# Weaving W1's units between W2's K tile pairs in a two-layer decoder trunk

## The chip, the cores and the metric

The kernel runs on one core of a Trainium2 chip. The metric is the time of one execution on the device, in microseconds (us). Five engines matter by name: TensorE (PE in the profile, its weight loads PEld), VectorE (DVE), ScalarE (ACT), GpSimd (POOL, almost unused) and SyncE (SP), which issues the DMAs. Each engine works through its own queue in order; semaphores tell it when an operand is there or a buffer free.

## The reference

Two decoder layers over 256 positions of width 2048, all in float32. Layer 0 mixes with a gated short convolution, layer 1 with multi-head latent attention; behind each mixer stands the same feed-forward block, and behind every sub-layer a layer norm of `alpha * x + f(x)`:

```python
def sq_relu_mlp(x, w1, w2):
    return jnp.square(jax.nn.relu(x @ w1)) @ w2
...
    h = layer_norm(ALPHA * h + mix, ln_g[layer, 0], ln_b[layer, 0])
    h = layer_norm(ALPHA * h + sq_relu_mlp(h, mlp_w1[layer], mlp_w2[layer]),
                   ln_g[layer, 1], ln_b[layer, 1])
```

W1 is 2048 x 8192 and W2 8192 x 2048. The change concerns this feed-forward block alone.

## The kernel before, in words

**Numbers in two parts.** TensorE multiplies in a rounded format (F32R). To keep float32's accuracy each operand is split: `split` (L125) casts the number to `hi` on ScalarE (L127) and takes the rest `lo` on VectorE (L128). A product is then hi by hi, hi by lo and lo by hi.

**Weights.** Every weight is read from memory once, as tiles of 128 x 1024 float32 (512 KB), in one fixed order, the list `stream`. `take` (L183) hands the next tiles to the matmuls and keeps `LOOK` = 5 preparation steps ahead. `prepare` (L141) does a step: a DMA on SP into one of `RAW` = 5 raw tiles, then the split into one of `WA` = 8 pairs of hi and lo tiles. So preparing weights is work for ScalarE and VectorE all through the kernel.

**The feed-forward block** (`mlp`, L575). The 8192 hidden columns are done in eight passes of 1024 (`NQ` = 8). A pass q has eight *units*: unit m is `x @ W1` for 128 hidden columns, 16 K tiles of one 512-column and one 256-column matmul (`mm_run`, L221: `high` L215 with the hi weights against x's hi and lo parts, `low` L219 with the lo weights). `whole` (L352) adds the two halves of the sum, ScalarE applies relu and square, and two units together are split into the tile `h`. In one K tile of a pass's first unit, number `TURNED` = 2, `low` stands ahead of `high`; that is the *turned* K tile.

The second half of the pass multiplies `h` by its 1024 rows of W2 and adds onto the running sums `acc`, 256 x 2048. The first and the last pass (q = 0, 7) do this plainly (`down`, L313). The middle passes (`FAST`, q = 1 to 6) use a Strassen-like scheme of **seven products** instead of eight: a *K tile pair* j (two hidden tiles) and a *column group* g (two of the four 512-column blocks) make a 2 x 2 by 2 x 2 block product, which `fast_products` (L343) does with seven accumulators named in `FACTORS` ("3", "1", "5", "7", "2", "6", "4"), each three matmuls (`dot`, L297: L300, L302, L303). For it, VectorE forms sums of the blocks of `h` (`form`, L703, into `sf` and `forms`), and `prepare` makes three split tiles and a half one out of two raw tiles, with one 1024-column and two 512-column differences (`raw_t` L162, L166, L169). The four accumulators in `OWN` have sums of their own (`sums`), which `fold` adds into `acc` after pass 6.

A middle pass is thus four pairs by two groups. Group 1 is done as `MIXED` = "sssp": three pairs by seven products and the fourth, the *plain* pair, by eight (`down_pairs`, L634), with one matmul cut in two (`EVEN`). Then group 0 is done, four pairs by seven products. In the profile the accumulators of group 1 are `ps_r`, those of group 0 `ps_f`, the units `ps_u`. A group's running sums are copied into the accumulators by ScalarE (`resumed`, L612; `resume` spreads those of group 1 over units 3 to 7), and copied back by ScalarE (`put_back`, L616) or added by VectorE (`keep`, L624).

The eight PSUM banks change roles from pass to pass: `busy` holds four banks for the units and part of the sums, `free` the other four.

In layer 0's last pass the next norm's preparation (`ln.prepare`, called by `begin`) goes along with the units; in layer 1 `turn_residual` (called by `extra`) transposes the residual behind the first unit of passes 1 to 4. The order on each engine follows the program's order as the tile framework schedules it; it moves independent instructions past each other.

Of the kernel before, what the change touches and what calls it, by code (L numbers as in the profile page):

```python
# [16 lines left out]
P = 128  # L17
# [20 lines left out]
MIXED = "sssp"  # L38
EVEN = (QC - 1, "22")
# [14 lines left out]
def trunk(ctx: ExitStack, tc: tile.TileContext, xT, vecs, lead, w_first, w_in, w_out, w_kv, w_q, w_uk, w_uv,  # L54
# [27 lines left out]

    def mlp_stream(l):
        out = []
        for q in range(NQ):
            out += halves(w1[l, q * QC:(q + 1) * QC])
            if q not in FAST:
                out += halves(w2[l, q])
                continue
            for j, kind in enumerate(MIXED):  # L90
                out += [(w2f[l, q, 1, j, 0], w2f[l, q, 1, j, 1])] if kind == "s" else \
                    halves(w2[l, q, 2, j]) + halves(w2[l, q, 3, j])
            out += [(w2f[l, q, 0, j, 0], w2f[l, q, 0, j, 1]) for j in range(QC // 2)]
        return out
# [480 lines left out]
    def mlp(idx, ln, blocks, fast, begin=None, extra=None, last=False):  # L575
# [32 lines left out]
        def resumed(p, g, name, bank):  # L608

            ps = psum(name, bank)  # L610
            if q != FAST[0] or p not in OWN:
                nc.scalar.copy(ps, place(p, g))  # L612
            return ps

# [3 lines left out]
        def keep(p, g, ps):  # L618

            at = place(p, g)  # L620
            if q == FAST[0] and p in OWN:
                nc.scalar.copy(at, ps)
            else:
                nc.vector.tensor_tensor(at, at, ps, ALU.add)  # L624

        def resume(busy, free, ps, m):

            b2, b3, b4, b6 = free
            b1, b5, b7, b22 = busy
            for p, bank in {3: (("3", b3),), 4: (("2", b2),), 5: (("4", b4), ("1", b1)), 6: (("6", b6), ("5", b5)),  # L630
                            7: (("7", b7), ("22", b22))}.get(m, ()):
                ps[p] = resumed(p, 1, f"ps_r{p}", bank)

        def down_pairs(h, forms, busy, free, ps):  # L634

            b2, b3, b4, b6 = free
            b1, b5, b7, b22 = busy
            new = set(OWN) if q == FAST[0] else set()
            onto = set(ps) - new
            for j, kind in enumerate(MIXED):  # L640
                if kind == "s":
                    last = j == MIXED.rindex("s")
                    fast_products(ps, h, forms, j, new if j == 0 else (), OWN if last else (), onto)
                    if last:
                        for p in OWN:
                            put_back(p, 1, ps[p])
                        then = {p: resumed(p, 0, f"ps_f{p}", bank) for p, bank in (("3", b1), ("1", b5))}
                    continue
                for two in (((0, "2"), (1, "4")), ((1, "22"), (0, "3"))):
                    w, = take(1, LOOK + 1)  # L650
                    for t, p in two:
                        for kk in range(2):
                            k = 2 * j + kk
                            dot(ps[p], wide_rows(w, kk), held(h[k], t), False, k == QC - 1, (k, p) == EVEN, True)
                    if j == len(MIXED) - 1:
                        if "5" not in then:
                            then.update({p: resumed(p, 0, f"ps_f{p}", bank) for p, bank in (("5", b7), ("7", b6))})
                        for _, p in two:
                            put_back(p, 1, ps[p])
            n = QC // 2  # L660
            onto = set(then) - new
            then.update({p: psum(f"ps_f{p}", bank) for p, bank in (("2", b2), ("6", b4), ("4", b22))})
            for j in range(n):
                fast_products(then, h, forms, j, set(then) - onto if j == 0 else (), then if j == n - 1 else (), onto)
            for p, _, _ in FACTORS:
                (put_back if p in onto or p in new else keep)(p, 0, then[p])
            return (b3, b1, b5, b7), (b6, b2, b4, b22)

        def fold():

            s1, s5, s7, s6 = (sums[:, i] for i in range(4))
            c = acc.rearrange("p t (g b c) -> p t b g c", g=2, b=2)
            for d, a, b in ((c[:, 0, 0], c[:, 0, 0], s1), (s6, s6, s1), (c[:, 0, 1], c[:, 0, 1], s6), (s7, s7, s6),
                            (c[:, 1, 0], c[:, 1, 0], s7), (c[:, 1, 1], c[:, 1, 1], s7),
                            (c[:, 0, 1], c[:, 0, 1], s5), (c[:, 1, 1], c[:, 1, 1], s5)):
                nc.vector.tensor_tensor(d, a, b, ALU.add)
                yield
# [8 lines left out]
        busy, free = (0, 1, 2, 3), (4, 5, 6, 7)  # L686
        for q in range(NQ):
            ht = act.tile([P, QC, 2 * T], F32R, tag="c", name=f"h{idx}_{q}")
            h = [ht[:, k, :] for k in range(QC)]
            forms = None  # L690
            if q in FAST:
                forms = act.tile([P, QC // 2, 2, 4 * P], F32R, tag="a2", name=f"forms{idx}_{q}")
            pair = []

            def pair_tile(m):

                if m % 2 == 0:
                    pool = (act, "ab") if m % 4 else (fast, "fp")
                    t = pool[0].tile([P, 2 * T], F32, tag=pool[1], name="fp")
                    pair.append(t.rearrange("p (i t) -> p i t", i=2))  # L700
                return pair[-1]

            def form(j):  # L703
                (a11, a21), (a12, a22) = ((pair[j][:, i, :P], pair[j][:, i, P:]) for i in range(2))
                sf = fast.tile([P, 4, P], F32, tag="sf", name="sf")
                s1, s2, s3, s4 = (sf[:, i, :] for i in range(4))
                nc.vector.tensor_tensor(s1, a21, a22, ALU.add)
                nc.vector.tensor_tensor(s3, a21, a11, ALU.subtract)
                nc.vector.tensor_tensor(s2, s1, a11, ALU.subtract)
                nc.vector.tensor_tensor(s4, a12, s2, ALU.subtract)  # L710
                split(forms[:, j, 0, :], forms[:, j, 1, :], sf.rearrange("p i c -> p (i c)"))

            def hidden(m, ps, evac, *func):
                both = pair_tile(m) if q in FAST else None
                f = both[:, m % 2, :] if both is not None else tmp.tile([P, T], F32, tag="fh", name="fh", bufs=3)
                evac(ps, f, *func)
                if not func:
                    nc.scalar.activation(f, f, AF.Relu)  # L718
                nc.scalar.activation(f, f, AF.Square)
                if both is None:  # L720
                    put_split(h[m], f)
                elif m % 2:
                    at = ht[:, m - 1:m + 1, :]
                    split(at[:, :, :T], at[:, :, T:], both)
                    form(m // 2)

            if q == 0:
                for m in range(QC):
                    if m < GROUP:
                        if m == 0:  # L730
                            ws = ln.ws if ln.ws else group_of(GROUP)
                            if not ln.ws:
                                mm_wide(ws, ln.xd)
                            ln.finish()
                        ps = ws[m][1]
                    else:
                        ws = [(take(), psum("ps_w"))]
                        mm_wide(ws, ln.xd)
                        ps = ws[0][1]
                    hidden(m, ps, ln.weighted, AF.Relu)  # L740
                acc = act.tile([P, 2, D], F32, tag="a1", name=f"acc{idx}")
            else:
                folds = fold()
                begun = {}
                for m, ps in enumerate(products(QC, xhl, TURNED, busy)):
                    hidden(m, ps, whole)
                    if extra and m == 0 and q <= NB:
                        for t in range(2):
                            extra(block, q - 1, t, busy[2 + t])
                    if q in FAST:  # L750
                        resume(busy, free, begun, m)
                    if q == NQ - 1:
                        next(folds, None)
                        if last and m >= QC - 2:
                            for t in range(2):
                                last_sum(m - QC + 2, t, free[2 * (m - QC + 2) + t])
# [19 lines left out]
    def to_wide(block, put, h):  # L776
# [10 lines left out]
        for n in range(NB):  # L787
            down(h, put, n)
            if n:
                turned(n - 1)  # L790
# [397 lines left out]
```

## Time and profile before

| what | value |
|---|---|
| median of three times | 1999.71 us (1998.16 to 2004.2) |
| span of the profiled execution | 1994.9 us, first to last instruction |
| the median over that span | 4.8 us; the profiled execution's own time is not listed beside its span |
| PE, DVE, ACT busy | 1987.7, 1709.4, 1354.9 us |
| DMA | 385.85 MB, mean 193 GB/s |
| the feed-forward passes 1 to 7 of layer 0 | from 452.78 to 997.46 us |
| of layer 1 | from 1394.56 us on |

In the rows, columns are start and length of an instruction, engine, line, operation, tile written and tiles read. A row of a stretch gives its length and then each engine's busy time with the number of instructions in brackets, the granted TensorE clock, the DMA share and GB/s. Matmuls are pipelined: their listed lengths overlap, so the start of the next one tells what one costs. To a lesser degree this holds for VectorE and ScalarE too.

### The profile page before, as it was taken

The numbers are of one execution on the slowest core, as the hardware profiler recorded it, in microseconds if no ns is written. First come the engines' busy times: TensorE is split into PE (matmuls) and PEld (weight loads), VectorE is DVE, ScalarE is ACT, GpSimd is POOL, SyncE is SP. The second block draws the span as 40 slices with busy tenths as digits, with TensorE's granted clock in tenths as the row PEclk, the third lists the DMA queues.
The fourth block names the chain that finished last, engine by engine and source line by source line (L and its number), as shares of the span: only waits on it lengthen the run. The fifth ranks groups of instructions, "written<-read, shape, count | busy, mean of one in ns | idle before, by whom it ended". The sixth has DMA issues, their size and how long they took to land.

```text
span 1994.9 us, 30180 instructions
## 1 busy us (share of the span) xinstructions
PE 1987.7 (100%) x11110; PEld 1737.2 (87%) x11110; DVE 1709.4 (86%) x2555; ACT 1354.9 (68%) x2154; POOL 2.3 (0%) x21
## 2 busy tenths in 40 slices
PE   9999999999999999999999999999999999999998
PEld 8888888988888888888889998898888888888886
DVE  8667667797999989989978988777899999999985
ACT  6444445586778778777756755558677787887772
POOL 0000000000000000000000000000000000000000
PEclk9999999999999999999999999999999999999999
DMA  8666666565657466574855543656464656656483
GB/s 318 205 191 187 190 190 190 179 193 157 212 170 251 148 216 221 177 243 147 281 171 159 170 140 123 201 180 195 146 233 155 232 161 220 222 178 233 150 269 130
DMA packets 106853, 385.85 MB, mean 193 GB/s; under 512 B 11857, under 2 KB 12625, under 8 KB 106449
## 3 DMA queue, kind: packets, MB, share of 16 engines
q1 hardware_dynamic: 106560, 383.79, 59.5%
q8 instruction: 87, 1.43, 0.3%
q14 instruction: 62, 0.50, 0.1%
q10 hardware_dynamic: 144, 0.13, 0.0%
HBM read 381.78 MB, written 2.10 MB: 192 GB/s over the span
## 4 chain that ended last, share of the span: by engine, by line
PE 98%; DVE 1%; ACT 1%; issue 0%; DVEq 0%; ACTq 0%
PE ps_u L215 20%; PE ps_l L215 13%; PE ps_u L219 10%; PE ps_l L219 7%; PE ps_f L300 4%; PE ps_f L303 4%; PE ps_f L302 4%; PE ps_r L303 4%; PE ps_r L302 4%; PE ps_r L300 4%; PE ps_d L300 2%; PE ps_d L302 2%; PE ps_d L303 2%; PE ps_w L249 2%; PE ps_w L248 2%; PE ps_w L247 2%
## 5 line engine op out<-in xcount | busy, mean ns | idle before, releaser
L128 DVE TENSOR_TENSOR lo<-raw,hi 128x1024 fp32r<-128x1024 f32 x710 | 861.8, 1220 | 190.6 <-ACT hi L127 119.9
L127 ACT CAST hi<-raw 128x1024 fp32r<-128x1024 f32 x710 | 741.8, 1051 | 247.4 <-PE ps_l L215 98.1
L215 PE MATMUL ps_u<-xhl,hi 128*128 128x512 f32 x1792 | 621.7, 392 | 0.0
L219 PE MATMUL ps_u<-xhl,lo 128*128 128x256 f32 x1792 | 498.2, 279 | 0.0
L215 PEld LDWEIGHTS ps_u<-xhl,hi 128*128 128x128 f32 x1792 | 334.5, 187 | 73.6 <-ACT acc L595 0.2
L219 PEld LDWEIGHTS ps_u<-xhl,lo 128*128 128x128 f32 x1792 | 338.1, 189 | 1.8
L215 PE MATMUL ps_l<-xhl_a,hi 128*128 128x512 f32 x704 | 244.1, 393 | 0.0
L219 PE MATMUL ps_l<-xhl_a,lo 128*128 128x256 f32 x704 | 195.4, 279 | 0.0
L215 PEld LDWEIGHTS ps_l<-xhl_a,hi 128*128 128x128 f32 x704 | 132.1, 188 | 29.9
L219 PEld LDWEIGHTS ps_l<-xhl_a,lo 128*128 128x128 f32 x704 | 131.9, 188 | 0.2
L127 ACT CAST hi_t<-raw_t 128x1024 fp32r<-128x1024 f32 x84 | 88.5, 1054 | 45.8 <-DVE raw_t L162 41.4
L162 DVE TENSOR_TENSOR raw_t<-raw,raw 128x1024 f32<-128x1024 f32 x84 | 102.3, 1218 | 1.8 <-DMA raw<-in_w2f_dram 1.5
L128 DVE TENSOR_TENSOR lo_t<-raw_t,hi_t 128x1024 fp32r<-128x1024 f32 x84 | 102.4, 1219 | 0.2
L718 ACT ACTIVATE fp<-fp 128x256 f32<-128x256 f32 x96 | 40.0, 416 | 63.2 <-DVE fp L356 62.6
L215 PE MATMUL ps_l<-z,hi 128*128 128x512 f32 x240 | 82.4, 391 | 0.0
L300 PE MATMUL ps_d<-hi,h 128*128 128x512 f32 x192 | 75.0, 391 | 0.0
L302 PE MATMUL ps_d<-lo,h 128*128 128x512 f32 x192 | 75.0, 390 | 0.0
L303 PE MATMUL ps_d<-hi,h 128*128 128x512 f32 x192 | 74.8, 389 | 0.0
L249 PE MATMUL ps_w<-xd,hi 128*128 128x258 f32 x256 | 72.7, 284 | 0.0
L248 PE MATMUL ps_w<-xd,lo 128*128 128x258 f32 x256 | 72.3, 282 | 0.0
L247 PE MATMUL ps_w<-xd,hi 128*128 128x258 f32 x256 | 72.3, 282 | 0.0
L215 PE MATMUL ps_l<-oT,hi 128*128 128x512 f32 x208 | 71.3, 391 | 0.0
(296 smaller groups left out, 3963.7 us busy)
## 6 DMA issues: line engine op xcount, KB each, us to landing
raw<-in_w_dram SPq DMA_DIRECT2D x344, 512.0 KB, 4.5
raw<-in_w2f_dram SPq DMA_DIRECT2D x168, 512.0 KB, 3.9
raw<-in_w_in_dram SPq DMA_DIRECT2D x88, 512.0 KB, 4.2
raw<-in_w_out_dram SPq DMA_DIRECT2D x32, 512.0 KB, 3.7
raw<-in_w_o_dram SPq DMA_DIRECT2D x32, 512.0 KB, 4.2
raw<-in_w_kv_dram SPq DMA_DIRECT2D x10, 512.0 KB, 3.7
raw<-in_w_q_dram SPq DMA_DIRECT2D x8, 512.0 KB, 4.0
raw<-in_w_uk_dram SPq DMA_DIRECT2D x8, 512.0 KB, 3.9
```

The lines of the kernel that those rows point to most:

```text
L127: nc.scalar.copy(hi, src)
L128: nc.vector.tensor_tensor(lo, src, hi.bitcast(F32), ALU.subtract)
L162: nc.vector.tensor_tensor(t.rearrange(two, a=2), b12.unsqueeze(1).to_broadcast([P, 2, BW]), r1.rearrange(two, a=2), ALU.subtract)
L215: nc.tensor.matmul(ps, w[blk // 8][0][:, blk % 8, :], x, start=first, stop=False)
L219: nc.tensor.matmul(ps[:, :T], w[blk // 8][1][:, blk % 8, :], x[:, :T], start=False, stop=last)
L247: nc.tensor.matmul(ps[:, :W], hi, x[k][:, :W], start=k == 0, stop=False)
L248: nc.tensor.matmul(ps[:, :W], lo, x[k][:, :W], start=False, stop=False)
L249: nc.tensor.matmul(ps[:, :W], hi, x[k][:, W:], start=False, stop=k == NC - 1)
L300: nc.tensor.matmul(ps, x[0], w[0], start=first, stop=False, skip_group_check=onto)
L302: nc.tensor.matmul(ps[:, at], x[0], w[1][:, at], start=False, stop=False, skip_group_check=onto)
L303: nc.tensor.matmul(ps, x[1], w[0], start=False, stop=last, skip_group_check=onto)
L718: nc.scalar.activation(f, f, AF.Relu)
```

## The change

**Order.** The units of a pass no longer stand together. From pass 1, unit 5 on, each unit is followed by one K tile pair of the seven-product work: `steps` yields (q, m, pair), where the pair is number m - 5 of the same pass for m = 5, 6, 7 and number m + 3 of the preceding pass for m = 0 to 4. So the pairs lag the units by `SHIFT` = 5. Five units ahead of the first pair and three behind the last stand alone. The stream of weights follows the same order: two tiles for a unit, then the two raw tiles of a pair.

**All pairs by seven products.** `PLAIN` is empty, so the plain pair and the cut matmul are gone; each of the 48 pairs of a layer takes `fast_products`. The branches for a plain pair are left in the code and unused.

**Turned tile.** `TURN` is true for every unit, so each unit of passes 1 to 7 has its third K tile turned.

**Banks and sums.** Seven banks hold the seven accumulators all through; all woven units share the eighth ("unit"), lone ones alternate between it and the bank of "6". The group changes once a pass: a group's last four pairs of one pass and first four of the next follow each other. At the change (`end`), all seven sums are put back and those of the other group resumed, all on ScalarE; `keep` is gone.

**Smaller moves.** `fold` works by group, 16 additions of 512 columns in place of 8 of 1024. Layer 0's preparations go with three lone units (chunks 1 to 9) and, chunks 10 to 15, into the block that follows. Layer 1's transposes go behind units 0 to 3 of pass 1. The function `to_wide` gains two lines for this.

The diff, cut to its core (helpers that only changed their place are left out):

```diff
-MIXED = "sssp"
-EVEN = (QC - 1, "22")
+PLAIN = ()
+SHIFT = 5
+
+
+def TURN(q, m):
+    return True
...
+    def steps():
+
+        for q in range(1, NQ):
+            for m in range(QC):
+                p, i = (q, m - SHIFT) if m >= SHIFT else (q - 1, m + QC - SHIFT)
+                yield q, m, (p, i // NB, i % NB, (p % 2) ^ (i // NB)) if p in FAST else None
...
     def mlp_stream(l):
-        out = []
-        for q in range(NQ):
-            out += halves(w1[l, q * QC:(q + 1) * QC])
...
+        out = halves(w1[l, :QC]) + halves(w2[l, 0])
+        for q, m, pair in steps():
+            out += halves(w1[l, q * QC + m])
+            if pair:
+                p, i, j, g = pair
...
+                    [(w2f[l, p, g, j, 0], w2f[l, p, g, j, 1])]
+        return out + halves(w2[l, NQ - 1])
...
+        base = Banks.count
+        bank = {p: (base + i) % 8 for i, p in enumerate(("6", "unit", "3", "1", "5", "7", "2", "4"))}
...
+        def resume(p, g, at=None):
+
+            ps[p] = psum(f"ps_{p}", bank[at or p])
+            onto.discard(p)
+            if p in OWN and begun[g] == FAST[0]:
+                fresh.add(p)
+            else:
+                nc.scalar.copy(ps[p], place(p, g))
+                onto.add(p)
...
+        def products_of(p, i, j, g):
...
+            end = i == 0 or p == FAST[-1]
...
+            fast_products(ps, h, forms, j, set(fresh), OWN if own else order if j == NB - 1 and end else (), onto)
+            fresh.clear()
...
+            elif j == NB - 1 and end:
+                begun[g] = 0
+                for o in order:
+                    put_back(o, g, ps[o])
+                    if i == 0:
+                        resume(o, 1 - g)
+            if p == FAST[-1] and j == NB - 1:
+                folds = chain(folds, fold(g))
+
+        for q, m, pair in steps():
+            lone = pair is None
+            if q == FAST[0] and m == SHIFT:
+                for o, _, _ in FACTORS:
+                    resume(o, 1)
+            w = take(2, LOOK + 1)
+            at = "6" if lone and m % 2 == 0 else "unit"
+            un = psum("ps_u", bank[at])
+            mm_run([(w, un)], xhl, 0, NC, NC, turned=TURNED if TURN(q, m) else None)
+            f = pair_tile(m)[:, m % 2, :]
+            whole(un, f)
+            nc.scalar.activation(f, f, AF.Relu)
+            nc.scalar.activation(f, f, AF.Square)
+            if extra and q == FAST[0] and m < NB:
+                for t in range(2):
+                    extra(block, m, t, spare[1 + (2 * m + t) % 3])
+            if q == NQ - 1:
+                for _ in range(3 if m >= SHIFT else 2):
+                    next(folds, None)
+                if begin and m >= SHIFT:
+                    begin(range(3 * (m - SHIFT) + 1, 3 * (m - SHIFT) + 4))
+            if pair:
+                products_of(*pair)
+            if m % 2:
+                finish_pair(m // 2)
...
+            if n < 2:
+                prepare_chunks(range(10 + 3 * n, 13 + 3 * n))
```

More of the change, by code (lines that the diff above doesn't have):

```diff
@@ L626, in resume @@
[L626 to L675, printed above, removed]
+        def fold(g):
+            s1, s5, s7, s6 = (sums[:, i, g, :] for i in range(4))
+            c = [[block(2 * g + b, t) for b in range(2)] for t in range(2)]
+            for d, a, b in ((c[0][0], c[0][0], s1), (s6, s6, s1), (c[0][1], c[0][1], s6), (s7, s7, s6),
+                            (c[1][0], c[1][0], s7), (c[1][1], c[1][1], s7), (c[0][1], c[0][1], s5), (c[1][1], c[1][1], s5)):
@@ L684, in last_sum @@
             nc.scalar.copy(finals[n, t], block(n, t))
[L686 to L690, printed above, removed]
-            if q in FAST:
[L692 to L737, printed above, removed]
@@ L738, in mlp, with finish_pair @@
+        def finish_pair(j):
+            both = fps.pop(j)
+            at = ht[:, 2 * j:2 * j + 2, :]
+            split(at[:, :, :T], at[:, :, T:], both)
+            if q in FAST:
+                form(j, both)
+        q = 0
+        for m in range(QC):
+            if m < GROUP:
+                if m == 0:
+                    ws = ln.ws if ln.ws else group_of(GROUP)
+                    if not ln.ws:
                         mm_wide(ws, ln.xd)
-                        ps = ws[0][1]
-                    hidden(m, ps, ln.weighted, AF.Relu)
@@ L741, in mlp @@
-                acc = act.tile([P, 2, D], F32, tag="a1", name=f"acc{idx}")
-            else:
[L743 to L756, printed above, removed]
-                        if begin:
-                            begin(range(max(2 * m, 1), 2 * m + 2))
@@ L760, in mlp @@
-            if q == NQ - 1 and last:
-                for i, (n, t) in enumerate(((2, 0), (3, 0), (2, 1), (3, 1))):
-                    last_sum(n, t, busy[i])
-                blocks(block, finals, h)
-                return
-            if q == NQ - 1:
-                blocks(block, put, h)
-                return
-            if q == 0:
-                for n in range(NB):
-                    down(h, put, n)
-                    if begin and n == 1:
-                        begin(range(1))
-            else:
-                busy, free = down_pairs(h, forms, busy, free, begun)
+                    ln.finish()
@@ new lines, in mlp @@
+                ps = ws[m][1]
+            else:
+                ws = [(take(), psum("ps_w"))]
+                mm_wide(ws, ln.xd)
+                ps = ws[0][1]
+            f = tmp.tile([P, T], F32, tag="fh", name="fh", bufs=3)
+            ln.weighted(ps, f, AF.Relu)
+            nc.scalar.activation(f, f, AF.Square)
+            put_split(h[m], f)
+        acc = act.tile([P, 2, D], F32, tag="a1", name=f"acc{idx}")
+        for n in range(NB):
+            down(h, put, n)
+            if begin and n == 1:
+                begin(range(1), (Banks.count + 4) % 8)
@@ new lines, in mlp @@
+        base = Banks.count
+        bank = {p: (base + i) % 8 for i, p in enumerate(("6", "unit", "3", "1", "5", "7", "2", "4"))}
+        spare = [bank[p] for p in ("3", "1", "5", "7", "2", "4", "6", "unit")]
+        forms = act.tile([P, QC // 2, 2, 4 * P], F32R, tag="a2", name=f"forms{idx}")
+        ps, onto, fresh = {}, set(), set()
+        folds = iter(())
+        def resume(p, g, at=None):
[6 more added lines that the diff above has]
+                onto.add(p)
@@ new lines, in mlp @@
+        for q, m, pair in steps():
[10 more added lines that the diff above has]
+            nc.scalar.activation(f, f, AF.Relu)
+            nc.scalar.activation(f, f, AF.Square)
+            if extra and q == FAST[0] and m < NB:
+                for t in range(2):
+                    extra(block, m, t, spare[1 + (2 * m + t) % 3])
+            if q == NQ - 1:
+                for _ in range(3 if m >= SHIFT else 2):
[6 more added lines that the diff above has]
+                finish_pair(m // 2)
+            if q == NQ - 1 and last and m >= QC - 2:
+                for t in range(2):
+                    last_sum(m - QC + 2, t, spare[2 * (m - QC + 2) + t])
@@ L776, in to_wide @@
+        for _ in folds:
+            pass
+        if last:
+            for i, (n, t) in enumerate(((2, 0), (3, 0), (2, 1), (3, 1))):
+                last_sum(n, t, spare[4 + i])
+            blocks(block, finals, h)
+            return
+        Banks.count = base + 2
+        blocks(block, put, h)
     def to_wide(block, put, h):
```

66 lines of the change are left out of this document (45 added, 21 removed).

## The prediction

> **What bounds the kernel now.** I read the page first, then busy time by stretch, then TensorE's rows in order of time at the borders of one pass, then the same for VectorE and ScalarE, and last the chain through the one pass that is longer than its neighbours.
>
> ```profile
> span 1994.9 us, 30180 instructions
> PE 1987.7 (100%) x11110; PEld 1737.2 (87%) x11110; DVE 1709.4 (86%) x2555; ACT 1354.9 (68%) x2154; POOL 2.3 (0%) x21
> ...
> PEclk9999999999999999999999999999999999999999
> ...
> raw<-in_w2f_dram SPq DMA_DIRECT2D x168, 512.0 KB, 3.9
> ```
>
> ```profile
> 619.23:702.46 83.23, 83.23 (x430) 71.27 (x428) 80.16 (x104) 67.44 (x103) 0.00 (x0) 1.00 0.64 207
> 868.91:953.06 84.15, 83.69 (x429) 71.12 (x428) 78.52 (x102) 66.34 (x103) 0.00 (x0) 1.00 0.59 198
> ```
>
> TensorE is never without work, at full clock. In a middle pass (columns: length, PE, PEld, DVE, ACT) VectorE is busy 80.16 of 83.23 us: two engines are nearly full at once. What a pass consists of is read from TensorE's starts:
>
> ```profile
> 273.06 0.40 PE L215 MATMUL ps_u<-z,hi 128*128 128x512 f32 x1
> ...
> 278.71 0.62 PE L215 MATMUL ps_l<-z,hi 128*128 128x512 f32 x2
> ...
> 619.23 0.39 PE L215 MATMUL ps_u<-xhl,hi 128*128 128x512 f32 x1
> ...
> 663.62 0.39 PE L300 MATMUL ps_r<-hi,forms 128*128 128x512 f32 x1
> ...
> 683.42 0.39 PE L300 MATMUL ps_f<-hi,forms 128*128 128x512 f32 x1
> ...
> 702.46 0.39 PE L215 MATMUL ps_u<-xhl,hi 128*128 128x512 f32 x1
> ...
> 708.02 0.39 PE L215 MATMUL ps_u<-xhl,hi 128*128 128x512 f32 x1
> ...
> 713.57 0.39 PE L215 MATMUL ps_u<-xhl,hi 128*128 128x512 f32 x1
> ```
>
> Eight W1 units take 44.39 us (619.23 to 663.62), the half of W2 with the plain pair 19.80, the half with four seven-product pairs 19.04, so 4.76 a pair. A unit is 5.55 us (708.02 to 713.57); the first of a pass, which has the turned K tile, 5.56; and one that starts fresh without a turned tile (273.06) 5.65.
>
> VectorE's and ScalarE's rows overlap: the next one starts before the listed end. So I cost them from start to start.
>
> ```profile
> 648.13 0.28 DVE L709 TENSOR_TENSOR sf<-sf,fp 128x128 f32<-128x128 f32 x1
> 648.33 1.22 DVE L128 TENSOR_TENSOR lo_t<-raw_t,hi_t 128x1024 fp32r<-128x1024 f32 x1
> 649.47 0.28 DVE L710 TENSOR_TENSOR sf<-fp,sf 128x128 f32<-128x128 f32 x1
> 649.67 0.42 DVE L356 TENSOR_TENSOR fp<-ps_u,t 128x256 f32<-128x256 f32 x1
> 650.00 0.68 DVE L128 TENSOR_TENSOR t<-raw,t 128x512 fp32r<-128x512 f32 x1
> 650.60 0.69 DVE L128 TENSOR_TENSOR forms<-sf,forms 128x512 fp32r<-128x512 f32 x1
> 651.21 1.22 DVE L162 TENSOR_TENSOR raw_t<-raw,raw 128x1024 f32<-128x1024 f32 x1
> ...
> 674.01 1.22 DVE L162 TENSOR_TENSOR raw_t<-raw,raw 128x1024 f32<-128x1024 f32 x1
> 675.27 0.69 DVE L166 TENSOR_TENSOR raw<-raw,raw_t 128x512 f32<-128x512 f32 x1
> 675.99 0.69 DVE L169 TENSOR_TENSOR raw<-raw 128x512 f32<-128x512 f32 x1
> ```
>
> ```profile
> 699.46 0.58 ACT L616 COPY acc<-ps_f 128x512 f32<-128x512 f32 x1
> 699.94 1.08 ACT L616 COPY sums<-ps_f 128x512 f32<-128x512 f32 x2
> 700.96 1.05 ACT L127 CAST hi<-raw 128x1024 fp32r<-128x1024 f32 x1
> 701.92 0.58 ACT L616 COPY sums<-ps_f 128x512 f32<-128x512 f32 x1
> ```
>
> VectorE steps: 1024 columns 1.135 us, 512 0.60, 256 0.335, 128 0.205, and 0.12 more when the next instruction reads the result (674.01 to 675.27 is 1.26). ScalarE: a sum's copy 0.50, a cast 0.96.
>
> **The change part by part.** *Plain pair to seven products* (12 places). TensorE saves 19.80 - 19.04 = 0.76 us each, 9.1 us, all on the path. VectorE pays for it: two splits (2.27) become three (3.41), one 1024-column difference (1.135) and three 512-column ones (1.80), 4.1 us more; the late adds L624 become ScalarE copies, 4 x 0.60 = 2.4 less. VectorE's steps of a pass: before, 39 splits and 7 differences of 1024 columns (52.2), 21 + 8 + 4 instructions of 512 (19.8), 8 of 256 (2.7), 16 of 128 (3.8 with their dependent steps) = 78.5. After: 40 + 8 of 1024 (54.5), 24 + 8 of 512 (19.2), 2.7, 3.8 = 80.2. DMA bytes stay as they are.
>
> *Turned tile in every unit.* From 7 to 56 units a layer: 49 x (5.57 - 5.55) = +1.0 us a layer. From below: nothing, if a unit behind a pair would run fast unturned; from above: if 21 matmuls, an odd number, leave TensorE in the slow cadence in spite of the turn, 0.10 us a unit, +10 for both layers. I take +2.0 for both, because the turned first units start just behind seven-product pairs.
>
> *Interleaving.* TensorE's step of one unit and one pair is 5.57 + 4.76 = 10.33 us, a pass 82.6. VectorE's 80.2 now stand beside it evenly, 10.0 in each step, where before the W1 half was light and the W2 half heavy. Two losses come with it.
>
> First, the raw tiles. A step draws five of five (two for the unit, three for the pair). In the order in which the changed program stands, the DMA of the next pair's first raw tile waits for the split of this pair's difference tile, its cast for the DMA, its split for the cast: 1.22 + 3.65 + 1.05 and some 0.2 of signals, 6.1 us from that split's start. VectorE has 5.48 us of other work there in every second step (splits of 1.135 three times, 0.60, 1.135 and 0.335) and 6.35 in the others. So it idles 0.65 in every second step, 2.6 a pass. The landing of 3.65 is an estimate, under the page's 3.9 because fewer DMAs are in flight; bounds: 0 (landing 3.0) and 5 a pass (landing 4.3).
>
> Second, the switch of column groups, once a pass. Seven sums are put back and seven resumed on ScalarE, 14 x 0.50 = 7.0 us. Before, the resumes were spread over units 3 to 7. In the program's order, some nine copies stand between the last cast of the pair behind the switch and the casts of the next unit. VectorE's next instruction is the following pair's difference, raw_t, which waits for a raw tile whose DMA can only start when this pair's last 1024-column split is through: 1.22 + 0.1 + 3.75 after it starts, 5.1, against 1.135 + 0.60 of work, so 3.4 us of idling. Queued behind it on VectorE are the splits of the next unit's two tiles and the sum of the finished unit (whole); TensorE's next unit waits for both. The nearest row for such a burst is the one pass that is too long:
>
> ```profile
> 927.47 0.93 issue
> 928.40 1.05 ACT hi L127
> 929.45 0.52 ACT t L127
> 929.96 1.45 ACT sums L616 x3
> 931.42 0.49 ACT ps_f L612
> 931.91 0.98 ACT hi L127
> 932.93 0.92 issue
> 933.86 1.10 ACT ps_f L612 x2
> 934.96 1.00 ACT acc L616 x2
> ```
>
> There raw-tile waits (the issue rows) and put-back copies in one chain stopped TensorE for 0.93 us (84.15 - 83.23 above). The bounds for the switch are thus 0.9 and 7.0; I take 3.4.
>
> What hides this is VectorE's distance to TensorE. A unit writes into one bank alone (four before), so whole must have read it before the next unit starts: 4.76 us of the pair less 0.335, 4.4. In the steady order VectorE is 1.7 us behind at the worse of two steps, which leaves 2.7. The pass has 82.6 - 80.2 = 2.4 to catch up, and the raw tiles use 2.6.
>
> *Moves.* Six of layer 1's residual preparations (256 columns, 0.335) go from the last pass into the block behind it, 2.0 us beside 11 us column blocks: 0, at most 2. Layer 2's residual transposes keep their number, as do the final folds (16 x 0.60 for 8 x 1.135, beside lone units): 0. SP's issues keep their number; their waits are the ones above.
>
> **The sum**, against the profiled execution of 1994.9. TensorE: -9.1 + 2.0 - 0.9 (the long pass) = -8.0. VectorE: 80.2 + 2.6 + 3.4 = 86.2 a pass against TensorE's 82.6, so 3.6 us of waiting a pass. Six switches a layer; the first follows four pairs and a full look-ahead, so five count, less the 2.7 in hand: 15.3 a layer, 30.6 in all. Span 1994.9 - 8.0 + 30.6 = 2017.5. The median of the three times, 1999.71, is 4.8 over this span, so 2022.
>
> The Trainium skill, "Perfetto Trace Analysis", Optimization Strategy, speaks for the change: where the most-contended engine changes from stage to stage, interleaving the stages may help. By that alone the sum is the first rival's. That the two halves do change over is in this trace; that interleaving gains is not.
>
> **The rivals.** *TensorE stays the bound.* VectorE's sum of 80.2 is under 82.6, and before, 78.5 of work, bursts and raw waits fitted under 83.2 without a stop in the pass shown, where VectorE's largest wait was this one (total, times, longest):
>
> ```profile
> DVE lo L128 <- ACT hi L127: 2.3, 5, 0.7
> ```
>
> It decides if the two idles together stay under 2.4 us a pass. Then 1999.7 - 8.0 = 1991.7: faster. Against it: five raw tiles in a step of five, and one unit bank.
>
> *Gain and waits cancel.* If the raw tiles cost nothing and the switch 3.4, VectorE needs 83.6 a pass, 1.0 over TensorE: 2 x (5 x 1.0 - 2.7) = 5, so about 1996 to 2001: no change.
>
> *The whole burst falls on VectorE.* With 7.0 at the switch in place of 3.4, ten times, +36: 2058. For it: ScalarE's queue is in order. Against it: in the order I see, the difference tile is drawn ahead of the blocked splits.
> The Trainium skill, "TensorE: Matmul & The Clock Gate", What's actually happening, adds that an idle window of about 3.4 us halves the clock for the next; by my estimate from that page ten such windows would cost some 17 us more. No run here shows it: the granted clock is full throughout.
>
> *The turn doesn't do what it says*, slow cadence: +8 on TensorE. It counts only in the first rival: 2000.
>
> **How the numbers follow.** The measurement tells about 0.3%, 6 us, from no change (1993.7 to 2005.7). Waiting VectorE (2006 to 2045, most likely 2022): 0.47. Burst in full (over 2045): 0.15. TensorE bound: 0.25 (faster). Cancelled, or TensorE bound with the slow cadence: 0.13. So faster 0.25, same 0.13, slower 0.62. The range takes in the first rival below and most of the last above: 1990 to 2055. My likeliest case alone is 2006 to 2045.
>
> **What would show it.** Right: VectorE over 95% busy in the middle passes, with raw_t waiting on a DMA and lo on hi at one place a pass; TensorE pausing at the first matmul of a unit behind a switch, released by VectorE (whole or lo); a pass of 85 to 87 us. Seven-product pairs at 4.76 and units at 5.57 show the first two parts right. Wrong: passes of 82.6 without pauses; units of 5.65; pauses at a pair's first product, released by the forms; or landings well over 4 us in the interleaved stretch.

## The result and the profile after

| | median, us | against the kernel before, same chip |
|---|---|---|
| before, beside the changed kernel | 2001.64 | |
| changed | 2019.77 (2017.34 to 2020.92) | 1.0101 [1.0089, 1.0113] |

The change costs 1.0%, some 20 us. The profiled execution took 2019.99 us with a span of 2018.2, 23.3 more than the span before (that profile is of a quick execution: by its span some 1997 us, where the four times beside the changed kernel run from 1998 to 2004). All of it lies in the two feed-forward blocks: layer 0's stretch from the first unit of pass 1 on went from 544.68 to 555.48 us, layer 1's from 547.21 to 559.85.

The page of the changed kernel (span and busy times, the shares of the chain that ended last, the group of VectorE's 1024-column difference with its idle time, the raw tiles' DMAs with the time to landing):

```profile
span 2018.2 us, 29835 instructions
PE 1993.9 (99%) x11062; PEld 1730.2 (86%) x11062; DVE 1730.0 (86%) x2589; ACT 1335.4 (66%) x2074; POOL 2.3 (0%) x21
...
PE 56%; DVE 24%; DMA 9%; issue 5%; ACT 5%; SPq 0%; DVEq 0%; ACTq 0%
...
L173 DVE TENSOR_TENSOR raw_t<-raw,raw 128x1024 f32<-128x1024 f32 x96 | 116.9, 1218 | 39.9 <-DMA raw<-in_w2f_dram 39.8
...
raw<-in_w2f_dram SPq DMA_DIRECT2D x192, 512.0 KB, 3.9
```

The same two lines of the kernel before, the chain and VectorE's difference:

```profile
PE 98%; DVE 1%; ACT 1%; issue 0%; DVEq 0%; ACTq 0%
...
L162 DVE TENSOR_TENSOR raw_t<-raw,raw 128x1024 f32<-128x1024 f32 x84 | 102.3, 1218 | 1.8 <-DMA raw<-in_w2f_dram 1.5
```

TensorE is still busy 99% by the page, yet its share of the chain fell from 98% to 56%. What took its place is above all VectorE (24%) and the landing of raw tiles (9%): `raw_t` waited 39.8 us for them, where it had waited 1.5 before.

Five stretches of layer 0, each of eight steps, from unit 6 of a pass to unit 6 of the next (length, PE, PEld, DVE, ACT, POOL, granted clock, DMA share, GB/s):

```profile
491.60:574.60 83.00, 83.00 (x425) 70.57 (x424) 76.63 (x101) 57.18 (x85) 0.00 (x0) 1.00 0.58 191
...
574.64:660.13 85.49, 83.81 (x426) 70.51 (x425) 80.08 (x104) 63.61 (x97) 0.00 (x0) 1.00 0.60 195
660.13:744.20 84.07, 83.47 (x426) 70.42 (x424) 79.31 (x103) 63.91 (x94) 0.00 (x0) 1.00 0.60 197
744.20:831.76 87.56, 85.07 (x426) 71.66 (x424) 80.93 (x105) 64.73 (x94) 0.00 (x0) 0.98 0.59 193
831.76:916.98 85.22, 83.59 (x426) 70.52 (x424) 80.34 (x105) 64.55 (x94) 0.00 (x0) 1.00 0.60 196
```

In the first TensorE is not held up, though its switch is in it. The other four, called passes from here on, take 84.1 to 87.6 us, 85.6 in the mean. Where TensorE is not held up, its starts show what it needs (first matmul of a unit, of a pair, of the next unit):

```profile
639.39 0.39 PE L226 MATMUL ps_u<-xhl,hi 128*128 128x512 f32 x1
...
644.96 0.39 PE L311 MATMUL ps<-hi,forms 128*128 128x512 f32 x1
...
649.76 0.39 PE L226 MATMUL ps_u<-xhl,hi 128*128 128x512 f32 x1
```

5.57 for a unit and 4.80 for a pair, so 83.0 a pass. Most of the 2.6 us above that is lost at pauses. The rows list only 1.6 a pass as idle, because a matmul listed with 0.39 us costs 0.23; from start to start the pauses of the four passes cost 8.5 of the 10.3 us, and a stretch of slow matmuls behind one of them (last section) 1.5. What TensorE waited for in the whole kernel (total, times, longest):

```profile
PE ps L311 <- ACT forms L138: 10.1, 8, 1.9
PE ps L313 <- DVE lo L139: 5.3, 9, 1.0
...
PE ps_u L226 <- DVE fp L367: 1.0, 3, 0.6
```

The pauses stand at the products of a pair (two of them in the last pass, 861.17 and 876.23), and hardly (1.0 us) at the first matmul of a unit. VectorE's rows at the switch of the last pass above, and its two largest groups by idle time in that pass:

```profile
865.89 1.22 DVE L139 TENSOR_TENSOR lo<-raw,hi 128x1024 fp32r<-128x1024 f32 x1
867.03 0.68 DVE L139 TENSOR_TENSOR t<-raw,t 128x512 fp32r<-128x512 f32 x1
871.55 1.23 DVE L173 TENSOR_TENSOR raw_t<-raw,raw 128x1024 f32<-128x1024 f32 x1 [3.83 <-DMA raw<-in_w2f_dram]
872.69 3.49 DVE L139 TENSOR_TENSOR lo<-raw,hi 128x1024 fp32r<-128x1024 f32 x3
```

```profile
L139 DVE TENSOR_TENSOR lo<-raw,hi 128x1024 fp32r<-128x1024 f32 x32 | 38.6, 1218 | 0.9 <-ACT hi L138 0.9
L173 DVE TENSOR_TENSOR raw_t<-raw,raw 128x1024 f32<-128x1024 f32 x9 | 11.0, 1217 | 3.8 <-DMA raw<-in_w2f_dram 3.8
```

The pass of 85.22 us is thus VectorE's: 80.34 of work, 3.8 of waiting for one raw tile at the switch, 0.9 spread over the raw-tile loop, and 0.2 of other gaps. While VectorE waited at the switch, ScalarE worked off its copies:

```profile
866.03 0.61 ACT L703 COPY ps<-acc 128x512 f32<-128x512 f32 x1
...
869.55 0.64 ACT L703 COPY ps<-sums 128x512 f32<-128x512 f32 x1
870.07 2.99 ACT L138 CAST hi<-raw 128x1024 fp32r<-128x1024 f32 x3
```

The cast that VectorE's next split needs begins at 870.07 and, at 1.0 us each, is through at about 871.1; the raw tile's DMA, in the chain of this stretch, landed at 871.42:

```profile
867.14 4.28 DMA raw<-in_w2f_dram
```

Two causes end within 0.3 us of each other there. The wait is put down to the later one; whether the other would have held VectorE as long is what the runs had to tell. Each layer has five such waits of 3.2 to 4.1 us; the last of its six switches has none.

### The profile page after: what moved, and what is told of

Read it like the earlier page. It is cut to its first block, busy times and chain, and to the rows that moved or that the text cites. A ratio compares the mean times of both kernels' runs of the same rounds, so it can differ in the third digit from the quotient of the medians.

```text
span 2018.2 us, 29835 instructions
## 1 busy us (share of the span) xinstructions
PE 1993.9 (99%) x11062; PEld 1730.2 (86%) x11062; DVE 1730.0 (86%) x2589; ACT 1335.4 (66%) x2074; POOL 2.3 (0%) x21
## 4 chain that ended last, share of the span: by engine, by line
PE 56%; DVE 24%; DMA 9%; issue 5%; ACT 5%; SPq 0%; DVEq 0%; ACTq 0%
PE ps_l L226 13%; DMA raw<-in_w2f_dram 8%; PE ps_l L230 7%; DVE lo L139 7%; PE ps_u L226 6%; DVE lo_t L139 4%; DVE raw_t L173 4%; PE ps_u L230 3%; ACT hi L138 2%; PE ps_d L311 2%; PE ps_d L313 2%; PE ps_d L314 2%; DVE raw L177 2%; DVE raw L180 2%; PE ps_w L260 2%
## 5 line engine op out<-in xcount | busy, mean ns | idle before, releaser
L230 PE MATMUL ps_u<-xhl,lo 128*128 128x256 f32 x1792 | 483.9, 280 | 0.0
L173 DVE TENSOR_TENSOR raw_t<-raw,raw 128x1024 f32<-128x1024 f32 x96 | 116.9, 1218 | 39.9 <-DMA raw<-in_w2f_dram 39.8
L138 ACT CAST hi_t<-raw_t 128x1024 fp32r<-128x1024 f32 x96 | 101.5, 1058 | 73.1 <-DVE raw_t L173 70.6
L139 DVE TENSOR_TENSOR lo_t<-raw_t,hi_t 128x1024 fp32r<-128x1024 f32 x96 | 117.1, 1220 | 1.1 <-ACT hi_t L138 0.8
L311 PE MATMUL ps<-hi,forms 128*128 128x512 f32 x192 | 76.3, 397 | 10.1 <-ACT forms L138 10.1
L313 PE MATMUL ps<-lo,forms 128*128 128x512 f32 x192 | 76.3, 397 | 5.3 <-DVE lo L139 5.3
L314 PE MATMUL ps<-hi,forms 128*128 128x512 f32 x192 | 75.9, 395 | 0.7 <-DVE forms L139 0.7
L313 PE MATMUL ps<-lo_t,forms 128*128 128x512 f32 x192 | 75.7, 394 | 0.0
L314 PE MATMUL ps<-hi_t,forms 128*128 128x512 f32 x192 | 75.6, 394 | 0.0
L314 PE MATMUL ps<-hi,h 128*128 128x512 f32 x192 | 75.5, 393 | 0.0
L313 PE MATMUL ps<-lo,h 128*128 128x512 f32 x192 | 75.2, 391 | 0.0
```

The lines of the kernel that those rows point to most:

```text
L138: nc.scalar.copy(hi, src)
L139: nc.vector.tensor_tensor(lo, src, hi.bitcast(F32), ALU.subtract)
L173: nc.vector.tensor_tensor(t.rearrange(two, a=2), b12.unsqueeze(1).to_broadcast([P, 2, BW]), r1.rearrange(two, a=2), ALU.subtract)
L230: nc.tensor.matmul(ps[:, :T], w[blk // 8][1][:, blk % 8, :], x[:, :T], start=False, stop=last)
L311: nc.tensor.matmul(ps, x[0], w[0], start=first, stop=False, skip_group_check=onto)
L313: nc.tensor.matmul(ps[:, at], x[0], w[1][:, at], start=False, stop=False, skip_group_check=onto)
```

## The experiments

The theory: with five raw tiles in a step that draws five, the raw tile for the pair behind a switch is asked for only after VectorE's own last split, VectorE stands idle, and with 80 us of work in a pass of 83 it has no room to make that up. Rivals: the double buffer `t4`; the weave as such; the seven products as such; ScalarE's burst of 14 copies at the switch. Ratios are against the kernel before on the same chip; the changed kernel is at 1.0101.

**Six raw tiles.** The room for the sixth (4 KB of each partition) comes from `t4`, which goes from two buffers to one.

```diff
-RAW, WA = 5, 8
+RAW, WA = 6, 8
...
-        f = state["fast"].tile([P, 2, BW], F32R, tag="t4", name=f"t4_{i}", bufs=2)
+        f = state["fast"].tile([P, 2, BW], F32R, tag="t4", name=f"t4_{i}", bufs=1)
```

> The changed kernel with six raw tiles in place of five; the room comes from one buffer for T4's parts in place of two. VectorE's order at the switch of column groups stays (the next pair's difference raw_t stands ahead of the next unit's splits), but the DMA it waits for may start one split (1.14 us) earlier, and the first raw tile of each pair long before its use. Theory A, VectorE lags because a step of five raw tiles draws on five: the wait of raw_t at a switch shrinks from 3.8 to about 2.7 us, the small waits of every second step go, VectorE gains some 2.5 us a pass against about 2.2 us of TensorE pauses a pass, so 1998 to 2004 us. Theory B, ScalarE's burst of put-back and resume copies is what stops VectorE: burst and order stay, so 2016 to 2021 us. Theory C, TensorE itself got slower by the weaving: 2016 to 2021 us.

Measured: 1997.53 us, 0.9996 [0.9986, 1.0005]. By stretch over the middle of both layers, with the changed kernel's rows ahead of those with six tiles:

```profile
574.64:985.00 410.36, 402.57 (x2037) 339.23 (x2036) 386.85 (x497) 308.68 (x454) 0.00 (x0) 1.00 0.59 195
1530.00:1945.00 415.00, 405.65 (x2055) 340.80 (x2054) 389.00 (x500) 310.97 (x455) 0.00 (x0) 1.00 0.59 194
```

```profile
574.64:985.00 410.36, 409.96 (x2095) 347.87 (x2094) 396.19 (x508) 315.05 (x468) 0.00 (x0) 1.00 0.62 204
1530.00:1945.00 415.00, 414.61 (x2124) 351.99 (x2123) 399.94 (x511) 321.10 (x478) 0.00 (x0) 1.00 0.63 207
```

TensorE's idle time falls from 7.8 and 9.4 us to 0.4 in each. VectorE is busier than with five tiles, 96.5% against 94.3% (396.19 and 386.85 of 410.36), and TensorE hardly stops. At a switch VectorE now shows:

```profile
861.40 1.23 DVE L173 TENSOR_TENSOR raw_t<-raw,raw 128x1024 f32<-128x1024 f32 x1 [1.92 <-DMA raw<-in_w2f_dram]
862.96 3.50 DVE L139 TENSOR_TENSOR lo<-raw,hi 128x1024 fp32r<-128x1024 f32 x3 [0.33 <-ACT hi L138]
```

1.92 for the tile and 0.33 for ScalarE's cast in place of 3.83. So one more raw tile takes back the whole loss, with the copies and VectorE's order at the switch as they were; the theory foretold it (the time is 0.5 us under its range). The run also uncovers ScalarE: the cast is late too.

**One `t4` buffer, five raw tiles**: the control for the run above, with only the second line of its edit.

> Control for the six raw tiles: five raw tiles, but T4's parts with one buffer. If that buffer matters, up to 5 us slower than the changed kernel; all theories expect no change, 2017 to 2022 us.

Measured: 2022.74 us, 1.0120 [1.0103, 1.0137]. Not faster than the changed kernel (and 0.7 us above the range expected), so the gain above is the raw tile's.

**The weave with the plain pair.**

```diff
-PLAIN = ()
+PLAIN = FAST
```

> The weaving without the twelve replaced pairs: PLAIN is the six middle passes, so the last pair of each group before a switch is done by eight products as before. VectorE's work of a pass falls by 4.1 us from 80.2 to 76.1, TensorE's rises by 0.76 to 83.4, and the put-backs are in two parts. Theory A: VectorE has over 7 us a pass in hand, pauses vanish, and what is left is the price of the weaving on TensorE (turned units +2, pairs of 4.80 for 4.76 some +3.5, less 0.9): 2003 to 2009 us. Theory B: two smaller bursts, about half of the pauses stay: 2010 to 2018 us.

Measured: 2002.76 us, 1.0021 [1.0012, 1.0031]. Its VectorE group and the middle of the two layers:

```profile
L173 DVE TENSOR_TENSOR raw_t<-raw,raw 128x1024 f32<-128x1024 f32 x84 | 102.6, 1222 | 42.8 <-DMA raw<-in_w2f_dram 42.1
```

```profile
574.64:985.00 410.36, 410.11 (x2094) 348.95 (x2094) 376.07 (x480) 306.69 (x467) 0.00 (x0) 1.00 0.62 204
1530.00:1945.00 415.00, 414.51 (x2123) 352.75 (x2122) 380.76 (x485) 312.00 (x476) 0.00 (x0) 1.00 0.63 205
```

VectorE waits for raw tiles as long in all as in the changed kernel (42.1 us), and TensorE is all but without pauses: VectorE has 376 us of work there, where it has 396 with six tiles and seven products. So a wait on VectorE need not cost anything where its work leaves room for it. The single waits are shorter here, though (35, the longest 2.6 us, against 14 and 4.1), and the put-backs come in two parts: how much of the gain is the room and how much the smaller burst, this run does not tell.

**Seven products alone**, in the order of the kernel before.

```diff
-MIXED = "sssp"
+MIXED = "ssss"
```

(and in `down_pairs` the branch for the plain pair, with its early resumes, taken out)

> The kernel before with its order kept and only the twelve plain pairs done by seven products. TensorE needs 9.1 us less; VectorE's work of a pass is 78.5 + 4.1 = 82.6 us beside TensorE's 82.5. Theory A: VectorE is then the bound in the second half of each pass and every wait counts, 2 to 5 us a pass: 2012 to 2045 us. If seven products cost nothing there and the loss comes from the weaving: 1990 to 1994 us.

Measured: 2052.03 us, 1.0272 [1.0257, 1.0287], above the range expected. TensorE waits for ScalarE and VectorE at the products of the second group:

```profile
PE ps_f L300 <- ACT hi_t L127: 16.2, 12, 1.7
PE ps_f L302 <- DVE t L128: 10.1, 12, 1.3
```

So seven products in every pair cost 2.7% in the old order, and the weave takes back 1.7 of it (1.0272 to 1.0101). The 2.7% is not the work's alone: without the plain pair the put-backs and resumes between the two groups stand together, a burst too.

**The same with six raw tiles** (the edit of the first run on top).

> The order of the kernel before, all pairs by seven products (2052 us with five raw tiles), now with six raw tiles. Theory A for that order: not a raw tile but work is short there, eight pairs in a row ask VectorE and ScalarE for more than TensorE's 4.76 us each; the sixth tile gives little: 2040 to 2052. If the raw tile were what stops it there too, as in the woven order, it would lose its pauses: under 2015.

Measured: 2043.84 us, 1.0231 [1.0216, 1.0246], as the theory had it for that order: eight pairs in a row ask for more preparation than TensorE's time holds, and a buffer does not make work shorter. In one half of a pass with W2, from 670.92 to 713.01, VectorE is busy 40.31 of the 42.09 us of the two groups, for which TensorE alone would need 38.1. Its one wait there, 1.44, is for a cast behind put-back copies, so ScalarE has a part here as well. Weaving and the sixth tile belong together: with seven products in every pair, either alone leaves 1.0% (woven, five) or 2.3% (not woven, six).

**The kernel before with six raw tiles** (the same two lines).

> The kernel before with six raw tiles and one t4 tile. In it TensorE never waits, so under theory A the sixth tile has nothing to give: 1996 to 2000, as before. If the sixth tile helped any order of this work, it would be under 1993.

Measured: 1999.20 us, 1.0006 [0.9997, 1.0016]. Nothing, as expected: where TensorE never waits, the tile has nothing to give.

**No resumed sums at a switch.**

```diff
-            if p in OWN and begun[g] == FAST[0]:
+            if begun[1 - g] == 0 or p in OWN and begun[g] == FAST[0]:
                 fresh.add(p)
```

> The changed kernel with five raw tiles, but at a switch of column groups the seven sums of the other group are not copied back into the accumulators: they start fresh, so the output is not the reference's, and ScalarE's burst at the switch falls from 14 copies to 7 (3.5 us less, 12 times). Theory A (the late raw tile starts the delay: its DMA waits for VectorE's own last split, not for ScalarE): raw_t still waits 3 us or more for the raw tile once a pass, VectorE stays the late one, and the time falls only by what ScalarE's part of the delay was: 2010 to 2020. Rival B (ScalarE's burst is the delay, the raw tile only shows it): the raw_t wait falls under 1.5 us, TensorE's pauses go, 1995 to 2004.

Measured: 2006.80 us, 1.0044 [1.0029, 1.0059]. Its waits on VectorE (total, times, longest), and the changed kernel's:

```profile
DVE lo L139 <- ACT hi L138: 101.1, 100, 5.2
...
DVE raw_t L173 <- DMA raw<-in_w2f_dram: 9.8, 8, 3.8
```

```profile
DVE lo L139 <- ACT hi L138: 84.7, 90, 5.2
...
DVE raw_t L173 <- DMA raw<-in_w2f_dram: 39.8, 14, 4.1
```

The raw-tile wait falls by 30.0 us with no raw tile added, and the wait for casts grows by 16.4: 13.6 less together, and the time fell by 13.0 (2019.77 to 2006.80). The time lies between the two ranges: that ScalarE has little part does not hold, nor that it has all of it. One reservation: with the copies gone VectorE's order at the switch is another one, `raw_t` stands behind the next unit's splits. So the run does not separate the copies' time from that order.

**No burst at all**: put-back left out as well, but for a layer's last pass.

```diff
                 for o in order:
-                    put_back(o, g, ps[o])
+                    if p == FAST[-1]:
+                        put_back(o, g, ps[o])
```

(on top of the edit above)

> The changed kernel with five raw tiles, and at a switch of column groups neither are the seven sums put back nor the other seven resumed, but for the last pass of a layer, which puts them back: 14 ScalarE copies less at most switches. The sums of the earlier passes are lost, so the output is not the reference's. What is left is the steady raw-tile loop alone (five raw tiles in a step of five). If that loop costs little, as the idle times of 0.3 to 0.4 us every second step say (1.5 us a pass, VectorE 81.7 against TensorE's 82.9 with pairs of 4.80), TensorE does not pause: 1995 to 1999. If the loop has a part of its own in the 22 us that the sixth raw tile gave, it stays over 2002.

Measured: 2001.53 us, 1.0021 [1.0012, 1.0031], just between the two ranges. The middle of the two layers:

```profile
574.64:985.00 410.36, 408.03 (x2082) 345.88 (x2081) 395.08 (x503) 276.74 (x399) 0.00 (x0) 1.00 0.62 202
1530.00:1945.00 415.00, 413.51 (x2118) 350.97 (x2117) 399.22 (x507) 283.33 (x412) 0.00 (x0) 1.00 0.63 205
```

TensorE idles 2.3 and 1.5 us, against 7.8 and 9.4 in the changed kernel and 0.4 and 0.4 with six tiles. So without the burst most of the loss is gone with five raw tiles (1.0101 to 1.0021). What is left against six tiles is 0.25%, some 5 us, 3 of them idle time in these two stretches (3.8 less 0.8); that would be the loop's part. The reservation of the last run holds here too: `raw_t` stands behind other splits in this run's order (after three of them, at 859.43), so that it is the copies' time which counts is likely, not shown. The revised theory: at a switch, VectorE is held by two things that end nearly together, the raw tile and the cast behind ScalarE's copies; taking away either brings it back to or near the 83 us that TensorE needs. For the raw tile the first run shows it.

**Six raw tiles, no turned tile.**

```diff
 def TURN(q, m):
-    return True
+    return False
```

(on top of the first run)

> Six raw tiles as in the run where TensorE does not pause (1997.5 us), and no unit has a turned K tile. If the turned tile is what sets the fast cadence behind a seven-product pair (21 matmuls, an odd number), a unit costs 5.65 instead of 5.57: 98 units by 0.08 us, +8, so 2003 to 2008. If the turn does nothing there, 1996 to 1999.

Measured: 2001.95 us, 1.0017 [1.0008, 1.0026]. The first matmuls of a unit, a pair and the next unit:

```profile
638.00 0.39 PE L226 MATMUL ps_u<-xhl,hi 128*128 128x512 f32 x1
...
643.64 0.40 PE L311 MATMUL ps<-hi,forms 128*128 128x512 f32 x1
...
648.43 0.39 PE L226 MATMUL ps_u<-xhl,hi 128*128 128x512 f32 x1
```

A unit takes 5.64 in place of 5.57, a pair 4.79 in place of 4.80. The turn is worth 4.2 us (1.0017 less 0.9996, of 2000), under the 8 expected. By the starts of both runs the 112 units need 631.1 us without it and 625.2 with it, 5.9 more, and the matmuls of the pairs 2.2 less. Without the turn 105 units take 5.63 us or more; with it 22 still do, 14 of them units with no pair directly ahead of them.

No version was faster than the kernel before; the woven order with six raw tiles and turned tiles equals it.

## Why the prediction was right, and where it was not

The time (2022 predicted, 2019.8 measured) and the engine that sets it came out as predicted. That the sum comes so close is luck, though: two of its terms were off by about 8 us each in opposite directions, and one step named the wrong place. The 4.8 us from span to median was too large as well: the executions listed with their spans are 1.7 to 2.8 over them (2019.99 and 2018.2), so the median of before belonged to slower executions than its profile. In spans, 2017.5 was predicted and 2018.2 measured.

*TensorE's term* (-8.0, a span of 1986.9 if nothing waits). Units at 5.57 are right for the woven ones, and so is the price of leaving the turn away (5.65 predicted, 5.64 measured). Pairs are 4.80, not 4.76: a pair's time had been read in a row of pairs, and between two units its first ten matmuls start 0.23 us apart and more, not 0.227. 96 pairs by 0.04 are 3.8 us. With six raw tiles, where VectorE hardly binds, the span is 1995.6, 8.7 above 1986.9. The pairs are 3.8 of it; the 96 steps of a unit and a pair take 1000.0 us, 4.5 above 96 times 10.37; and twelve of the units without a pair take 5.63 to 5.65 in spite of the turn, 0.9 more. These are 9.2 in all, 0.5 too many, which is not accounted for. So the first rival's own number, 1991.7, would not have been reached either: with the wait gone, the change gains nothing.

*VectorE's work* (80.2 a pass): 80.34 measured, right.

*The switch* (3.4 us for the raw tile): 3.8 over a pass, 39.8 in all. The chain is the one predicted, a DMA that starts at 867.14, when the pair's last 1024-column split (865.89, 1.22 long) is through, and lands 4.28 later; the estimate had a landing of 3.75. Five switches a layer were counted; five have the wait, and the first of them costs TensorE nothing (83.00 of 83.00), as predicted. The working saw ScalarE's copies ahead of the next unit's casts but did not time them: the cast was due at nearly the same moment.

*The raw-tile loop* (2.6 a pass): 0.9 of waiting for casts in the pass shown, 0.9 to 2.4 in the four. Oversized: the working let VectorE idle 0.65 at every second step, and the rows behind the switch show less:

```profile
894.45 1.23 DVE L139 TENSOR_TENSOR lo<-raw,hi 128x1024 fp32r<-128x1024 f32 x1 [0.17 <-ACT hi L138]
...
914.92 1.23 DVE L139 TENSOR_TENSOR lo<-raw,hi 128x1024 fp32r<-128x1024 f32 x1 [0.34 <-ACT hi L138]
```

From the split of the difference tile (888.72, 909.02) to these two the loop takes 5.73 and 5.90 us, not 6.1; its DMAs landed in 3.37 and 3.55, where 3.65 was estimated.

A pass thus came to 85.6 against 83.0 (86.2 against 82.6 predicted): 2.6 a pass, not 3.6. Between six tiles and five the span grows by 22.6 (1995.6 to 2018.2) where 30.6 was predicted for the waits: 8.0 too large, against the 8.7 that TensorE's term was too small. The row on which the lower bound of the switch rested, 0.93 us of TensorE stopped in the long pass, lists 0.46 of it as idle (83.69 busy of 84.15).

*The place.* This step failed. The prediction put TensorE's pauses at the first matmul of the unit behind a switch, through the single unit bank; those waits are 1.0 us in all. Most of the waiting is at a pair's products that need the `forms` (10.1 us), most of the rest at a pair's weights (5.3). In the pass shown the first pause comes ahead of the switch's wait (VectorE stands still from 867.7 on), and only the second behind it:

```profile
861.17 0.49 PE L311 MATMUL ps<-hi,forms 128*128 128x512 f32 x1 [0.87 <-ACT forms L138]
...
876.23 0.50 PE L313 MATMUL ps<-lo,forms 128*128 128x512 f32 x1 [0.76 <-DVE lo L139]
```

The second is near what was predicted: released by VectorE's `lo`, two matmuls ahead of a unit (876.80). The first is not. VectorE has little to catch up with in a pass, so its lag stays and, as we read it, shows where an operand has the least lead: the last pair of `h`, whose forms are made just one step before they are used. ScalarE adds to it: the sum for the forms was through at 860.07, a put-back copy ran from 860.00, and the cast of the forms began at 860.48. Six of the eight pauses at the forms have this, 0.37 to 0.65 us each, at most 2.9 of the 10.1.

The prediction had listed pauses released by the forms as a sign against itself; the lag was as predicted, most of its place was not. Its other sign, VectorE over 95% busy, points the wrong way: 94.3% with pauses, 96.5% without.

*The rivals.* TensorE as the bound is what six raw tiles make of it, but not five. The full burst on VectorE did not come: the wait at a switch stayed under 4.2 us. That ScalarE's queue has a large part in the lag, which this rival said, the two runs without copies make likely, with the reservation on VectorE's order made there.

## What to carry over

Where two engines are nearly full, add up the second one's work and its waits in one pass and compare that with the first one's time: a busy share alone would have named the wrong kernel here. Weaving two stages evens out the work but also ties each step's buffers together; count the tiles that a step draws against those that exist, because one more can be worth the whole loss, and little or nothing in another order. And a wait that the profile puts down to one releaser may hide a second; here it ended 0.3 us earlier.

## What was not expected of the hardware

After one pause TensorE ran slower for a while (in the pass with a granted clock of 0.98; from 775.4 to 779.2 it was 0.58):

```profile
775.48 0.49 PE L311 MATMUL ps<-hi,forms 128*128 128x512 f32 x1 [1.92 <-ACT forms L138]
...
776.49 0.63 PE L313 MATMUL ps<-lo_t,forms 128*128 128x512 f32 x1
776.91 0.63 PE L314 MATMUL ps<-hi,forms 128*128 128x512 f32 x1
```

From 776.06 to 779.05 the starts are 0.43 us apart, not 0.23, about 1.5 us lost. The Trainium skill, "TensorE: Matmul & The Clock Gate", What's actually happening, has the clock halve after an idle window of about 3.4 us. Here 1.92 us sufficed once, and in the run without resumed sums a longer idle of 2.43 us did not slow what followed (0.23 to 0.24 us between starts, a granted clock of 1.00):

```profile
1638.62 0.50 PE L311 MATMUL ps<-hi,forms 128*128 128x512 f32 x1 [2.43 <-ACT forms L138]
1638.96 0.40 PE L313 MATMUL ps<-lo,forms 128*128 128x512 f32 x1
1639.20 0.39 PE L311 MATMUL ps<-hi,h 128*128 128x512 f32 x1
```

The run with seven products alone has eight pauses of 1.71 us each: over the 8 us from their end on the granted clock was 0.79 after five of them (by estimate 1.7 us lost each) and 1.00 after three. So the length of a pause alone does not decide. What does was not tried and stays open.
